# In a two-pass matmul stream, the order of the first few upper and lower products after each change of stage

## Chip, cores and metric

One core of a Trainium2 chip runs the whole kernel. The metric is the device time of one execution in microseconds. A change of under about 0.2% (5 us here) cannot be told from none by a measurement of this kernel.

## What is computed

Two decoder layers on 256 tokens of width 2048, all in float32. The first layer mixes tokens by dilated attention, the second by a gated sum of compressed, selected and windowed attention over shared keys and values. Each is followed by a squared-ReLU MLP of width 8192 and a gated per-layer embedding. Cut to what carries the time:

```python
for i in range(2):
    hn = rmsnorm(h, attn_norm_g[i])
    h = h + (dilated_mixture_attention(hn, a_w_in[i], a_w_out[i]) if i == 0 else
             nsa_attention(hn, b_w_qg[0], b_w_out[0], *shared))   # shared: k/v from rmsnorm(h, kv_norm_g) @ w_kv_shared
    hn = rmsnorm(h, mlp_norm_g[i])
    h = h + square(relu(hn @ mlp_w1[i])) @ mlp_w2[i]               # 2048 -> 8192 -> 2048
    gate = sigmoid(rmsnorm(h, ple_norm_g[i]) @ ple_w_gate[i])
    h = h + (p[i] @ ple_w_proj[i]) * gate
return rmsnorm(h, final_norm_g)
```

## The kernel before

Weights come in chunks of 128 x 1024 float32 (512 KB), one DMA each. ScalarE rounds a chunk to `whi` (L202), VectorE takes the rest, `wlo` = raw - `whi` (L208). Activations are split in the same way, and a tile `xa` (or `oT`, `ko`, `pg`, `h`) holds both parts side by side: 256 columns of upper part, 256 of lower part. A product of float32 accuracy is then made of products of rounded parts, in one of two ways.

- **Feature-major** stages (`quad`, `single`) take a 128 x 128 piece of weights as the stationary operand, twice. `mm_tiles` issues, for each piece, an **upper** product (L332: `whi` against all 512 columns) and a **lower** one (L336: `wlo` against the 256 upper columns). I call the two a pair. With `run=1` they alternate; with `run=2` the order is upper, upper, lower, lower; with `run=8` eight uppers and then eight lowers; with a negative run each lower follows `-run` uppers later. A chunk holds eight pairs.
- **Token-major** stages (`token_major`, L446, L447, L448) take activations as the stationary operand and stream 512 columns of weights in every product, three for each piece.

A `quad` makes four 128-row tiles of output over all its chunks (8 pairs a chunk); a `single` makes one over two chunks. The program is one list of steps, written out in advance; the matmuls run in that order and everything else is placed around them. `prog.op` places a step between chunks.

Where the two kinds of stage meet:

- Mixer A: a unit of values (`v_unit`, token-major, 8 chunks) stands ahead of heads 0, 1, 2, 4 and 5. A head has six tiles by `single` (i = 0 to 5). After the first chunk of tile 1 comes `a_scores` (fp32 products, L748 and L749), after the first chunk of tile 3 `a_transpose` (L777 to L780), and after tile 4 `a_pv` (L800 to L805).
- `out_proj`: four quads in a row, moving operand `oT` or `ko`; the first quad has `a_pv` or `b_pv` steps between its chunks. MLP block 0 follows at once.
- `mlp`: four blocks of 2048 hidden features for each layer; a block is four up-projection quads (256 pairs) and then four token-major down-projection units. Block 0 has the norm's small products after its fifth chunk (L241 and L265). Blocks 1 to 3, called the later blocks here, begin right behind a token-major product.
- Mixer B's sixteen queries: a `single` each, with `b_pv` (L1242 to L1244) and `b_transpose` (L1218) between its two chunks and `b_scores` (L1169 to L1171) behind it.

In the kernel before, three tables choose how a feature-major stage starts after a token-major one. `OPENINGS[layer][block]` is (width of an fp32 product put in front, run of the first chunk, run of the rest); `UNIT_OPENINGS[u]` is (width, run of the first chunk) for the head behind value unit u. `opening(n)` (L356) issues one fp32 product with n columns whose output nobody reads; it shows as two products in the trace.

```python
OPENINGS = (((0, 1, 1), (T, 1, 1), (P, 1, 1), (0, 8, 1)),
            ((0, 1, 1), (0, 2, 1), (0, 2, 2), (0, -1, 1)))
UNIT_OPENINGS = {1: (1, 1), 2: (0, 4), 3: (64, 1), 4: (0, 8)}
```

So block 1 of the first layer opens with a 256-column fp32 product, block 2 with a 128-column one, block 3 with a run of eight; in the second layer block 1 has its first chunk in twos, block 2 all chunks in twos, block 3 the staggered order. Head 1 opens with a 1-column product, head 2 with a run of four, head 4 with a 64-column product, head 5 with a run of eight, and head 0 with nothing.

Of the kernel before, what the change touches and what calls it, by code (L numbers as in the profile page):

```python
# [30 lines left out]
ROPE_SWAP = [(j + 16) % 32 for j in range(32)]  # L31

WARM_UP = 14

OPENINGS = (((0, 1, 1), (T, 1, 1), (P, 1, 1), (0, 8, 1)),
            ((0, 1, 1), (0, 2, 1), (0, 2, 2), (0, -1, 1)))

UNIT_OPENINGS = {1: (1, 1), 2: (0, 4), 3: (64, 1), 4: (0, 8)}
DMA_AHEAD = 7
SPLIT_AHEAD = 3  # L40
RAW_BUFS, HI_BUFS, LO_BUFS = 4, 6, 5
# [96 lines left out]
def kernel(ctx: ExitStack, tc: tile.TileContext, a: dict, out: bass.AP):  # L138
# [185 lines left out]
    def mm_tiles(hi, lo, tiles, run=1):  # L324

        def upper(t):  # L330
            ps, col, rhs, first, _ = t
            nc.tensor.matmul(ps, hi[:, col:col + P], rhs, start=first, stop=False)  # L332

        def lower(t):
            ps, col, rhs, _, last = t
            nc.tensor.matmul(ps[:, :T], lo[:, col:col + P], rhs[:, :T], start=False, stop=last)  # L336

        if run < 0:
            for n, t in enumerate(tiles):
                upper(t)  # L340
                if n + run >= 0:
                    lower(tiles[n + run])
            for t in tiles[run:]:
                lower(t)
            return
        for n in range(0, len(tiles), run):
            for t in tiles[n:n + run]:
                upper(t)
            for t in tiles[n:n + run]:
                lower(t)  # L350

    def opening(n):

        def go():
            ps = banks2()[:, 0, :] if parity[0] else bank()
            nc.tensor.matmul(ps[:, :n], ones, xp[0][:, :n], start=True, stop=True)  # L356
        prog.op(go)

    def sum_halves(ps):
        s = tmp.tile([P, T], F32, tag="es", name="es", bufs=4)  # L360
# [15 lines left out]
            yield  # L376
        yield from g

    def quad(src, nk, acts, done, hooks=None, single_ring=False, late=False, runs=(1, 1)):

        st = []
        for c in range(nk // 2):
            def step(hi, lo, c=c):
                if c == 0:
                    st.extend([bank() for _ in range(4)] if single_ring else four_banks())
                for i in range(2):
                    have(acts, 2 * c + i)
                mm_tiles(hi, lo, [(st[f], i * 512 + f * P, acts[2 * c + i], 2 * c + i == 0, 2 * c + i == nk - 1)
                                  for f in range(4) for i in range(2)], runs[c > 0])
                if c < nk // 2 - 1:  # L390
                    return []
                return [delayed(done(f, st[f]), f // 2 if late else 0) for f in range(4)]
            prog.chunk(src(c), step)
            for fn in (hooks or {}).get(c, ()):
                prog.op(fn)

    def single(src, acts, done, mid=(), ring=bank, one_half=False, run=1):

        st = []
        for c in range(2):  # L400
            def step(hi, lo, c=c):
                if c == 0:
                    st.append(ring())
                tiles = []
                for i in range(8):
                    k = 8 * c + i
                    if one_half:
                        xg, ps = have(acts, k), st[0][:, :T]
                        wh, wl = hi[:, i * P:(i + 1) * P], lo[:, i * P:(i + 1) * P]
                        nc.tensor.matmul(ps, wh, xg[:, :T], start=k == 0, stop=False)  # L410
                        nc.tensor.matmul(ps, wh, xg[:, T:], start=False, stop=False)
                        nc.tensor.matmul(ps, wl, xg[:, :T], start=False, stop=k == KT - 1)
                        continue
                    tiles.append((st[0], i * P, have(acts, k), k == 0, k == KT - 1))
                mm_tiles(hi, lo, tiles, 1 if c else run)
                return [done(st[0])] if c else []
            prog.chunk(src(c), step)
            if c == 0:
                for fn in mid:
                    prog.op(fn)  # L420
# [67 lines left out]
    def out_proj(src, nk, oT, gi, to, norm, hooks, single_ring):  # L488
        for q in range(4):
            def done(f, ps, q=q):  # L490
                add_to_x(4 * q + f, ps)
                yield
                yield from renorm(4 * q + f, gi, to, norm)
            quad(lambda c, q=q: src[q * (nk // 2) + c], nk, oT, done, hooks if q == 0 else None,
                 single_ring and q == 0, True)
            if q == 0 and single_ring:
                prog.op(lambda: parity.__setitem__(0, 1))

    def mlp(layer, xg, norm, to, norm2):

        def down(b, q, ps0, ps1, mm):
            c = slice(q * 512, (q + 1) * 512)
            if b == q == 0:
                cur["y"] = cur["h"].tile([P, 2, D], F32, name=f"y{layer}")
            y = cur["y"]
            for j, ps in enumerate((ps0, ps1)):
                if b:
                    nc.vector.tensor_add(y[:, j, c], ps, y[:, j, c])
                else:
                    nc.scalar.copy(y[:, j, c], ps)  # L510
            if b < NFB - 1:
                return
            yield
            yield "tensor"
            tr = two_banks(not mm)
            for f in range(4):
                for j in range(2):
                    k = 4 * q + f
                    nc.tensor.transpose(tr[f // 2][:, (f % 2 * 2 + j) * P:(f % 2 * 2 + j + 1) * P],
                                        y[:, j, k * P:(k + 1) * P], ident)  # L520
            yield
            for i in range(2):
                nc.vector.tensor_add(xp[2 * q + i], tr[i], xp[2 * q + i])
            for i in range(2):
                yield
                both = [renorm(4 * q + 2 * i + f, G_PLE + layer, to, norm2) for f in range(2)]
                for g in both:
                    next(g)
                yield
                for g in both:  # L530
                    next(g, None)

        for b in range(NFB):
            h = [None] * 16
            fp32, first, rest = OPENINGS[layer][b]
            if fp32:
                opening(fp32)
            for q in range(4):
                def done(f, ps, q=q, h=h):
                    t = sum_halves(ps)  # L540
                    yield
                    while norm.r is None:
                        yield
                    nc.vector.scalar_tensor_tensor(t, t, 0.0, norm.rb, op0=ALU.max, op1=ALU.mult)
                    yield
                    nc.scalar.activation(t, t, AF.Square)
                    ht = cur["h"].tile([P, 2 * T], F32R, tag="h", name="h", bufs=20)
                    yield from split_to(ht, t)
                    h[4 * q + f] = ht
                base = layer * 128 + (b * 4 + q) * 8  # L550
                quad(lambda c, base=base: a["w1"][base + c], KT, xg, done,
                     {4: [norm.factor]} if b == 0 and q == 0 else None, late=True,
                     runs=(rest if q else first, rest))
            for q in range(4):
                base = layer * 128 + (b * 4 + q) * 8
                token_major(lambda c, base=base: a["w2"][base + c], h,
                            lambda ps0, ps1, mm, b=b, q=q: down(b, q, ps0, ps1, mm), whole=True)
# [257 lines left out]
    hooks[4].append(tables)  # L815
    v_unit(0, hooks, banks2)
    prog.op(lambda: nc.vector.tensor_add(pair, ident[:, :64], ident[:, 64:]) and None)
    last_unit = [None]
    for h in range(HA):
        for i in range(6):  # L820
            if i == 0:
                fp32, run = UNIT_OPENINGS.get(last_unit[0], (0, 1))
                last_unit[0] = None
                if fp32:
                    opening(fp32)
            single(lambda c, h=h, i=i: a["w_qk"][(h * 6 + i) * 2 + c], x_a0,
                   lambda ps, h=h, i=i: qk_done(h, i, ps), run=run if i == 0 else 1, mid=
                   [lambda h=h: a_scores(h - 1)] if h and i == 1 else
                   [lambda h=h: a_transpose(h - 1)] if h and i == 3 else
                   [lambda i=i: square_pair(2 * i)] if not h and i < 4 else ())  # L830
# [9 lines left out]
                       7: []})  # L840
        elif u:
            v_unit(u)
            last_unit[0] = u
    out_proj(a["w_oA"], HA, oT, G_MLP, x_m0, n_m0,
             {0: [lambda: a_pv(HA - 2, True)], 1: [lambda: a_pv(HA - 1, True)]}, True)
    prog.op(lambda: close_pool("A"))
# [405 lines left out]
    for h in range(HB):  # L1252
        mid = [lambda h=h: b_pv(h - 4)] if h >= 4 else []
        if h >= 3:
            mid.append(lambda h=h: b_transpose(h - 3))
        single(lambda c, h=h: a["w_q"][2 * h + c], x_a1, lambda ps, h=h: q_done(h, ps), mid)
        if h:
            prog.op(lambda h=h: b_scores(h - 1))
    hooks = {0: [lambda: b_pv(HB - 4, True), lambda: b_transpose(HB - 3)],
# [111 lines left out]
```

## Time and profile before

| | |
|---|---|
| median of 3 runs | 2520.42 us (2520.09 to 2520.87) |
| the profiled execution's own time | 2519.85 us |
| its span, first to last instruction | 2517.8 us |
| granted TensorE clock | 0.999 |
| PE busy | 2506.4 us (100%), 13505 products |
| VectorE busy, ScalarE busy | 1661.9 us (66%), 1351.5 us (54%) |
| DMA | 466.10 MB, 185 GB/s |

In the rows of the timeline the first number is the start of the first instruction in us from the span's start, the second the time from there to the end of the last one; products overlap, so how fast they follow one another is read from the starts. A row of a table by stretches gives the stretch, its length, the time that PE was busy in it with the number of products that touch it, the granted clock, and the DMA engines' share and rate.

### The profile page before, as it was taken

The page shows a single profiled execution, that of the slowest core. Times are in us where ns is not written, and L with a number is a line of the kernel's source. Part 1 is how long each engine was busy: PE and PEld are TensorE (multiplying, and loading weights), DVE is VectorE, ACT ScalarE, POOL GpSimd, SP SyncE. Part 2 cuts the span into 40 slices and gives each one's busy share as a digit, 9 for nine tenths or more (in the row PEclk, how much of TensorE's full clock was granted, in tenths as well). Part 3 has the DMA queues.
Part 4 walks back from the last instruction along what each step waited for, and adds up shares of the span by engine and source line. Part 5 has one row for each costly group of instructions (what it writes and reads, how often), then busy time and mean ns, then how long its engine had stood idle before and what let it go on. Part 6 is the DMA issues. An engine that isn't in the chain of part 4 may idle for free.

```text
span 2517.8 us, 36100 instructions
## 1 busy us (share of the span) xinstructions
PE 2506.4 (100%) x13505; PEld 2160.0 (86%) x13505; DVE 1661.9 (66%) x2808; ACT 1351.5 (54%) x2168; POOL 10.4 (0%) x24
## 2 busy tenths in 40 slices
PE   9999999999999999999999999999999999999998
PEld 8888888888888888888888889888888888888887
DVE  6766677865465565566787989866546556556677
ACT  6444444554454453455564788755545445445455
POOL 0000000000000000000000000000000000000000
PEclk9999999999999999999999999999999999999999
DMA  7555545555555555555555743455555555555553
GB/s 271 171 181 177 176 160 180 176 188 192 190 191 192 191 186 193 190 187 185 190 193 188 245 162 120 142 190 190 192 193 189 193 191 189 192 192 187 184 185 123
DMA packets 130111, 466.10 MB, mean 185 GB/s; under 512 B 14608, under 2 KB 15888, under 8 KB 129936
## 3 DMA queue, kind: packets, MB, share of 16 engines
q1 hardware_dynamic: 129264, 462.68, 53.7%
q8 instruction: 105, 1.72, 0.3%
q0 software_dynamic: 528, 1.07, 0.2%
q14 instruction: 70, 0.57, 0.1%
q10 hardware_dynamic: 144, 0.07, 0.0%
HBM read 461.65 MB, written 2.10 MB: 184 GB/s over the span
## 4 chain that ended last, share of the span: by engine, by line
PE 99%; DVE 0%; DMA 0%; SPq 0%; ACT 0%; issue 0%; DVEq 0%
PE mm L332 22%; PE at L332 17%; PE mm L336 11%; PE at L336 9%; PE mm L448 6%; PE mm L447 6%; PE mm L446 6%; PE at L448 5%; PE at L446 5%; PE at L447 5%; PE at L1218 0%; PE at L749 0%; PE mm L1242 0%; PE mm L976 0%; PE mm L977 0%; DMA raw<-in_w_v 0%
## 5 line engine op out<-in xcount | busy, mean ns | idle before, releaser
L208 DVE TENSOR_TENSOR wlo<-raw,whi 128x1024 fp32r<-128x1024 f32 (+1 forms) x875 | 1065.4, 1219 | 640.3 <-PE at L448 131.6
L202 ACT CAST whi<-raw 128x1024 fp32r<-128x1024 f32 (+1 forms) x875 | 919.9, 1052 | 882.1 <-PE mm L332 204.7
L332 PE MATMUL mm<-xa,whi 128*128 128x512 f32 x2176 | 761.0, 397 | 0.0
L336 PE MATMUL mm<-xa,wlo 128*128 128x256 f32 x2176 | 593.3, 279 | 0.0
L332 PE MATMUL at<-xa,whi 128*128 128x512 f32 x1648 | 572.0, 394 | 0.0
L332 PEld LDWEIGHTS mm<-xa,whi 128*128 128x128 f32 x2176 | 403.6, 188 | 88.4 <-issue 0.4
L336 PE MATMUL at<-xa,wlo 128*128 128x256 f32 x1648 | 450.0, 279 | 0.0
L336 PEld LDWEIGHTS mm<-xa,wlo 128*128 128x128 f32 x2176 | 409.1, 189 | 6.7
L332 PEld LDWEIGHTS at<-xa,whi 128*128 128x128 f32 x1648 | 304.3, 187 | 65.5
L336 PEld LDWEIGHTS at<-xa,wlo 128*128 128x128 f32 x1648 | 310.8, 189 | 5.8
L446 PE MATMUL at<-whi,h 128*128 128x512 f32 x512 | 199.5, 390 | 0.0
L446 PE MATMUL mm<-whi,h 128*128 128x512 f32 x512 | 199.4, 389 | 0.0
L448 PE MATMUL mm<-wlo,h 128*128 128x512 f32 x512 | 199.3, 389 | 0.0
L447 PE MATMUL mm<-whi,h 128*128 128x512 f32 x512 | 199.2, 389 | 0.0
L448 PE MATMUL at<-wlo,h 128*128 128x512 f32 x512 | 199.2, 389 | 0.0
L447 PE MATMUL at<-whi,h 128*128 128x512 f32 x512 | 199.2, 389 | 0.0
L446 PEld LDWEIGHTS mm<-whi,h 128*128 128x128 f32 x512 | 96.1, 188 | 20.0
L448 PEld LDWEIGHTS mm<-wlo,h 128*128 128x128 f32 x512 | 96.1, 188 | 19.9
L448 PEld LDWEIGHTS at<-wlo,h 128*128 128x128 f32 x512 | 96.1, 188 | 19.9
L447 PEld LDWEIGHTS at<-whi,h 128*128 128x128 f32 x512 | 96.1, 188 | 19.9
L446 PEld LDWEIGHTS at<-whi,h 128*128 128x128 f32 x512 | 96.1, 188 | 19.8
L447 PEld LDWEIGHTS mm<-whi,h 128*128 128x128 f32 x512 | 96.1, 188 | 19.7
(317 smaller groups left out, 2533.2 us busy)
## 6 DMA issues: line engine op xcount, KB each, us to landing
raw<-in_w SPq DMA_DIRECT2D x512, 512.0 KB, 3.5
raw<-in_w_qk SPq DMA_DIRECT2D x96, 512.0 KB, 3.5
raw<-in_w_gate SPq DMA_DIRECT2D x56, 512.0 KB, 4.2
raw<-in_w_kv SPq DMA_DIRECT2D x48, 512.0 KB, 4.3
raw<-in_w_v SPq DMA_DIRECT2D x46, 512.0 KB, 3.6
raw<-in_w_q SPq DMA_DIRECT2D x32, 512.0 KB, 4.3
raw<-in_w_oB SPq DMA_DIRECT2D x32, 512.0 KB, 3.6
raw<-in_w_oA SPq DMA_DIRECT2D x16, 512.0 KB, 3.5
```

What stands on the lines that cost most here:

```text
L202: nc.scalar.copy(hi[:, c], t[:, c])
L208: nc.vector.tensor_sub(lo[:, c], t[:, c], f32(hi)[:, c])
L332: nc.tensor.matmul(ps, hi[:, col:col + P], rhs, start=first, stop=False)
L336: nc.tensor.matmul(ps[:, :T], lo[:, col:col + P], rhs[:, :T], start=False, stop=last)
L446: nc.tensor.matmul(st[j], xh, wh, start=k == 0, stop=False)
L447: nc.tensor.matmul(st[j], xl, wh, start=False, stop=False)
L448: nc.tensor.matmul(st[j], xh, wl, start=False, stop=k == KT - 1)
```

## The change

Both tables and `opening` go. The first chunk of blocks 1 to 3 of either MLP runs in twos and all other MLP chunks in ones. The first chunk of tile 0 of heads 0, 1, 2, 4 and 5 runs in twos. In `out_proj` the first chunk of the second quad runs in twos, in both layers. And of mixer B's queries the even ones run both their chunks in twos, through a new argument `both`. Every engine but PE keeps its list of instructions in the same order; on PE the upper and lower products are the same 4272 and 4272 calls, and the four fp32 openings are gone.

```diff
-OPENINGS = (...)
-UNIT_OPENINGS = {...}
+UNIT_AHEAD = (0, 1, 2, 4, 5)
...
     def mm_tiles(hi, lo, tiles, run=1):
...
-        if run < 0:
-            ...
         for n in range(0, len(tiles), run):
-            for t in tiles[n:n + run]:
-                upper(t)
-            for t in tiles[n:n + run]:
-                lower(t)
-    def opening(n):
-        ...
+            for ps, col, rhs, first, last in tiles[n:n + run]:
+                nc.tensor.matmul(ps, hi[:, col:col + P], rhs, start=first, stop=False)
+            for ps, col, rhs, first, last in tiles[n:n + run]:
+                nc.tensor.matmul(ps[:, :T], lo[:, col:col + P], rhs[:, :T], start=False, stop=last)
...
# quad
-                                  for f in range(4) for i in range(2)], runs[c > 0])
+                                  for f in range(4) for i in range(2)], 1 if c else run)
# single
-                mm_tiles(hi, lo, tiles, 1 if c else run)
+                mm_tiles(hi, lo, tiles, run if c == 0 or both else 1)
# out_proj
-                 single_ring and q == 0, True)
+                 single_ring and q == 0, True, 2 if q == 1 else 1)
# mlp
-                     runs=(rest if q else first, rest))
+                     run=2 if b and not q else 1)
# heads of mixer A
-                if fp32:
-                    opening(fp32)
...
-                   lambda ps, h=h, i=i: qk_done(h, i, ps), run=run if i == 0 else 1, mid=
+                   lambda ps, h=h, i=i: qk_done(h, i, ps), run=2 if i == 0 and h in UNIT_AHEAD else 1, mid=
# queries of mixer B
-        single(lambda c, h=h: a["w_q"][2 * h + c], x_a1, lambda ps, h=h: q_done(h, ps), mid)
+        single(lambda c, h=h: a["w_q"][2 * h + c], x_a1, lambda ps, h=h: q_done(h, ps), mid,
+               run=2 - h % 2, both=True)
```

More of the change, by code (lines that the diff above doesn't have):

```diff
@@ L33 @@
 WARM_UP = 14
-OPENINGS = (((0, 1, 1), (T, 1, 1), (P, 1, 1), (0, 8, 1)),
-            ((0, 1, 1), (0, 2, 1), (0, 2, 2), (0, -1, 1)))
-UNIT_OPENINGS = {1: (1, 1), 2: (0, 4), 3: (64, 1), 4: (0, 8)}
+UNIT_AHEAD = (0, 1, 2, 4, 5)
 DMA_AHEAD = 7
@@ L324, in mm_tiles @@
     def mm_tiles(hi, lo, tiles, run=1):
[L330 to L336, printed above, removed]
-        if run < 0:
-            for n, t in enumerate(tiles):
-                upper(t)
-                if n + run >= 0:
-                    lower(tiles[n + run])
-            for t in tiles[run:]:
-                lower(t)
-            return
-        for n in range(0, len(tiles), run):
-            for t in tiles[n:n + run]:
-                upper(t)
-            for t in tiles[n:n + run]:
-                lower(t)
-    def opening(n):
[L354 to L357, printed above, removed]
+        for n in range(0, len(tiles), run):
+            for ps, col, rhs, first, last in tiles[n:n + run]:
+                nc.tensor.matmul(ps, hi[:, col:col + P], rhs, start=first, stop=False)
+            for ps, col, rhs, first, last in tiles[n:n + run]:
+                nc.tensor.matmul(ps[:, :T], lo[:, col:col + P], rhs[:, :T], start=False, stop=last)
     def sum_halves(ps):
@@ L377, in delayed, with quad @@
         yield from g
-    def quad(src, nk, acts, done, hooks=None, single_ring=False, late=False, runs=(1, 1)):
+    def quad(src, nk, acts, done, hooks=None, single_ring=False, late=False, run=1):
         st = []
@@ L395, in quad, with single @@
                 prog.op(fn)
-    def single(src, acts, done, mid=(), ring=bank, one_half=False, run=1):
+    def single(src, acts, done, mid=(), ring=bank, one_half=False, run=1, both=False):
         st = []
@@ L534, in mlp @@
             h = [None] * 16
-            fp32, first, rest = OPENINGS[layer][b]
-            if fp32:
-                opening(fp32)
             for q in range(4):
@@ L817 @@
     prog.op(lambda: nc.vector.tensor_add(pair, ident[:, :64], ident[:, 64:]) and None)
-    last_unit = [None]
     for h in range(HA):
         for i in range(6):
[L821 to L825, printed above, removed]
             single(lambda c, h=h, i=i: a["w_qk"][(h * 6 + i) * 2 + c], x_a0,
-                   lambda ps, h=h, i=i: qk_done(h, i, ps), run=run if i == 0 else 1, mid=
+                   lambda ps, h=h, i=i: qk_done(h, i, ps), run=2 if i == 0 and h in UNIT_AHEAD else 1, mid=
                    [lambda h=h: a_scores(h - 1)] if h and i == 1 else
@@ L842 @@
             v_unit(u)
-            last_unit[0] = u
     out_proj(a["w_oA"], HA, oT, G_MLP, x_m0, n_m0,
```

## The prediction

> **What bounds the kernel now.** I read the page's busy table first, then the list of waits on PE.
>
> ```profile
> PE 2506.4 (100%) x13505; PEld 2160.0 (86%) x13505; DVE 1661.9 (66%) x2808; ACT 1351.5 (54%) x2168; POOL 10.4 (0%) x24
> ```
> ```profile
> PE mm L681 <- DVE ones L174: 1.1, 1, 1.1
> PE at L448 <- DVE wlo L208: 0.5, 1, 0.5
> ```
>
> PE is never without work: its two longest waits in the whole execution are 1.1 and 0.5 us, once each. So no wait can be removed, and nothing that the other engines do faster would count. What is left is how closely products follow one another. A busy PE says nothing about that, so the third view is the table by stretches, one stretch for each later MLP block, from the start of the last L448 product ahead of it to the start of the first L446 product behind it.
>
> ```profile
> 666.72:756.14 89.42, 89.42 (x516) 1.00 0.55 189
> 843.00:933.90 90.90, 90.90 (x516) 1.00 0.54 186
> 1020.72:1111.35 90.63, 90.63 (x515) 1.00 0.54 187
> 1869.78:1958.75 88.97, 88.97 (x514) 1.00 0.55 190
> 2045.58:2134.97 89.39, 89.39 (x515) 1.00 0.56 189
> 2221.79:2312.45 90.66, 90.66 (x514) 1.00 0.55 187
> sum 539.97, PE 539.97; mean PE 90.00
> ```
>
> The six do the same 256 pairs on tiles of the same shapes, at the same granted clock (1.00), yet take 88.97 to 90.90 us. The differences follow the way each starts. The fourth row is block 1 of the second layer, the one whose first chunk already runs in twos. Without the 0.23 us of its last L448 it makes 88.74 / 256 = 0.3466 us a pair. The last row (staggered start) makes 90.43 / 256 = 0.3533. These are two rhythms that each keep going to the end of the block once they have begun: chunk borders, quads and the change from the `mm` to the `at` banks don't break them. I call them fast and slow. The third row (run of eight) and the second (128-column opening) are slow as well. The first (256-column opening) is fast, and its 0.45 us over the fourth row is what its opening costs. The fifth has all chunks in twos: (89.39 - 0.23) / 256 = 0.3483, so twos themselves are not the fastest order; what pays is one chunk of them, and ones after it.
>
> The timeline shows the two starts in twos, and one opening:
>
> ```profile
> 1869.78 0.39 PE L448 MATMUL at<-wlo,h 128*128 128x512 f32 x1
> 1870.00 0.61 PE L332 MATMUL mm<-xa,whi 128*128 128x512 f32 x2
> 1870.46 0.40 PE L336 MATMUL mm<-xa,wlo 128*128 128x256 f32 x2
> 1870.69 0.63 PE L332 MATMUL mm<-xa,whi 128*128 128x512 f32 x2
> ...
> 1872.78 0.40 PE L332 MATMUL mm<-xa,whi 128*128 128x512 f32 x1
> ```
> ```profile
> 2045.58 0.39 PE L448 MATMUL at<-wlo,h 128*128 128x512 f32 x1
> 2045.80 0.62 PE L332 MATMUL mm<-xa,whi 128*128 128x512 f32 x2
> 2046.26 0.40 PE L336 MATMUL mm<-xa,wlo 128*128 128x256 f32 x2
> ```
> ```profile
> 843.00 0.40 PE L448 MATMUL at<-wlo,h 128*128 128x512 f32 x1
> 843.23 0.38 PE L356 MATMUL mm<-x,ones 128*128 128x128 f32 x2
> 843.37 0.48 PE L332 MATMUL mm<-xa,whi 128*128 128x512 f32 x1
> 843.68 0.28 PE L336 MATMUL mm<-xa,wlo 128*128 128x256 f32 x1
> ```
>
> Read the starts: both starts in twos go 0.22, 0.46 us. The same start gives the same steps, so I take the rhythm for a consequence of the order at the start and not of chance. Eight pairs in twos take 1872.78 - 1870.00 = 2.78 us. The opening stands for 843.37 - 843.23 = 0.14 us, and the upper behind it for 0.31 where one behind an L448 takes 0.23 or so (in the first listing, half of the 0.46 of two).
>
> **The change part by part.** *The later MLP blocks.* All six get the order of the fourth row, behind the same kind of stage, from the same ring of banks, over the same sixteen `xa` buffers. 6 x 88.97 = 533.82 against 539.97: **-6.15 us**. The new order asks for the first `wlo` one product later than before, so it adds no wait; PE's list is the only one that changes. The cover for the faster pace is in the fourth row too: DMA brought 190 GB/s there and PE did not wait. If VectorE or the DMAs fell behind, it would show first there, and it does not.
>
> *The five heads behind a value unit.* Stretches from the last L448 to the head's first score product (24 pairs), and for head 0 to its norm (72 pairs):
>
> ```profile
> 85.74:94.66 8.92, 8.92 (x52) 1.00 0.74 247
> 145.88:154.44 8.56, 8.56 (x50) 1.00 0.50 183
> 243.93:252.85 8.92, 8.92 (x53) 1.00 0.49 174
> 304.07:312.72 8.65, 8.65 (x51) 1.00 0.50 180
> 29.21:54.87 25.66, 25.66 (x146) 1.00 0.73 243
> ```
>
> In twos and then fast ones, 24 pairs take 0.23 + 2.78 + 16 x 0.3466 = 8.56, which the run of four (head 2) has already. So head 1 and 4 gain 0.36 each, head 5 gains 0.09, head 2 nothing. Head 0 gets 0.23 + 2.78 + 64 x 0.3466 = 25.19, a gain of 0.47. Together **-1.3 us**. All eight pairs of a head write one bank, those of the MLP four; I cost that at nothing, since the run of eight came out slow from one bank (head 5: 8.42 / 24 = 0.351) and from four.
>
> *What follows in a head.* The fp32 score and transpose products break the rhythm, and which one comes after depends on what stood before, in a way that the trace shows but I cannot derive:
>
> ```profile
> 168.41:176.81 8.40, 8.40 (x51) 1.00 0.50 178
> 206.39:214.96 8.57, 8.57 (x52) 1.00 0.51 174
> 178.55:192.43 13.88, 13.88 (x83) 1.00 0.45 156
> 374.95:389.08 14.13, 14.13 (x82) 1.00 0.42 152
> ```
>
> These are the 24 pairs behind the transposes of heads 2 (fast) and 3 (slow), and the 40 behind a later value product, fast and slow. If heads 1, 2, 4 and 5 all turned slow there, it would cost 4 x 0.17 + 2 x 0.25 + 2 x 0.1 (sixteen pairs at 0.0067) = +1.4; if heads 3 and 6 turned fast, -0.7. I take **0**, for four of the six are fast now.
>
> *The second output quad, and mixer B's queries.* Neither start has a counterpart before.
>
> ```profile
> 452.00:489.00 37.00, 37.00 (x214) 1.00 0.52 183
> 1625.50:1693.00 67.50, 67.50 (x386) 1.00 0.57 191
> 495.00:504.00 9.00, 9.00 (x53) 1.00 0.53 181
> ```
>
> Two products of each count overlap the ends, so the pace is 37.0 / 106 = 0.349 a pair in the first output projection, 67.5 / 192 = 0.3516 in the second, and 9.0 / 25.5 = 0.353 in the first chunks of the MLP behind it. The change can touch 96, 192 and twice 40 pairs. All of them fast: 96 x 0.0024 + 192 x 0.005 + 80 x 0.0064 = -1.7. All slow: 96 x 0.0043 + 192 x 0.0017 = +0.7. Since these paces are neither of the two, something in `oT` and `ko` as operands keeps disturbing the rhythm, and a good start would soon be lost: I take **-0.2**.
>
> ```profile
> 1455.24:1461.00 5.76, 5.76 (x33) 1.00 0.83 261
> 1471.91:1474.78 2.87, 2.87 (x18) 1.00 0.48 176
> 1475.05:1477.98 2.93, 2.93 (x18) 1.00 0.16 32
> 1488.63:1491.45 2.82, 2.82 (x19) 1.00 0.20 83
> 1493.41:1496.27 2.86, 2.86 (x19) 1.00 0.53 180
> ```
>
> These are both chunks of query 0 (16 pairs), the two of query 2, the two of query 4. A chunk in twos takes 2.78, or about 2.86 behind the transposes, where the first upper follows an fp32 product as behind an opening (+0.08). Query 0: -0.20; query 2: -0.16; queries 4 to 14: some 0.03 each, -0.2. Sum **-0.5**. Should twos lock slow there, 8 x 0.3533 = 2.83 makes +0.05 in 16 chunks, +0.3 in all; should the odd queries gain 0.04 a chunk as well, -1.1.
>
> **Sum.** -6.15 - 1.3 + 0 - 0.2 - 0.5 = -8.2, from the profiled execution's 2519.85 (span 2517.8 and 2.05 outside it, which doesn't change) to 2511.7. The median of the runs, 2520.42, stands 0.57 above that execution, so I predict 2512.2. The bounds of the three open terms reach 2.8 below it (0.7 + 1.5 + 0.6) and 3.1 above (1.4 + 0.9 + 0.8).
>
> A rule speaks against all of this. The Trainium skill, "TensorE: Matmul & The Clock Gate", section "Back-to-back issue gap", gives a warm product N / 2.4 + 2.5 ns after the one before, whatever the order: 215.8 + 109.2 = 325 ns a pair, an estimate from that page. The trace disagrees: 346.6 in one block and 353.3 in another of the same shapes.
>
> **Rivals.** *The order does not matter and the rhythm is set elsewhere* (by that rule, for one). Then only the openings go: 3 x (0.14 + 0.08) + 0.45 = 1.1, and the median is 2519.3. Against it stand six blocks with one work and different times. Chance 0.04.
>
> *The start in twos locks fast in some blocks only*, because the fourth row owes its rhythm to something else that it starts with. Each block that turns slow costs 90.66 - 88.97 = 1.69. With two slow the gain falls to 4.8 us, under 0.2% (5.04 us, about what a measurement can tell from none); with three, to 3.1: 2515.6 to 2517.3. Against it: the start in twos of the fifth row runs through the same steps. Chance 0.08.
>
> *Slower than before:* the start in twos locks slow everywhere else, as one run of eight did in two places. Six blocks at 90.66 make 543.96, +4.0; heads at 0.3533 make 0.23 + 24 x 0.3533 = 8.71 and -0.2 in sum, head 0 none. That is 2523.7 on the profiled scale, 2524.2 on the median's, and 2525.2 with the bad bounds of queries and output quads. From five slow blocks on the whole gain is gone (8.2 / 1.69 = 4.9). Chance 0.04.
>
> **How the numbers follow.** My forecast has 0.80, and 0.04 is left for mixtures such as one slow block, still faster. Range: 2509.4 (the good bounds) to 2516.0 (the bad bounds at 2515.3, and two slow blocks). Faster by over 0.2% (below 2515.4): 0.80 and most of the mixtures, with a part of the second rival, 0.86. Within: the rest of that rival, the first, and most of the third, 0.12. Slower by over 0.2%: 0.02.
>
> **What would show it.** Right: six blocks of 88.97, whatever their layer; first chunks at 0.22, 0.46; scores of heads 1 and 4 8.56 after the last L448; no PE wait longer than before. Wrong: a later block near 90.66 with the same first chunk, which would make the rhythm depend on more than the order; queries in twos above 2.83 a chunk; a wait of PE on `whi` or `wlo` inside a block.

## The result and the profile after

The median fell from 2520.27 to 2513.70 us (10 runs each), a ratio of 0.9974 with a 95% interval of 0.9966 to 0.9983: 6.6 us faster, where 8.2 was forecast. The profiled span went from 2517.8 to 2511.3.

The busy table after says as little as before; the waits on PE are the same few:

```profile
PE 2500.4 (100%) x13497; PEld 2156.5 (86%) x13497; DVE 1662.3 (66%) x2808; ACT 1351.0 (54%) x2168; POOL 10.4 (0%) x24
```
```profile
PE mm L650 <- DVE ones L170: 1.1, 1, 1.1
PE at L420 <- DVE wlo L204: 0.4, 1, 0.4
PE at L1131 <- DVE ko L450: 0.3, 1, 0.3
```

There are eight products fewer (the four openings, two records each) and no new wait. Lines have moved: L327 and L329 are now the upper and lower product, L418 to L420 the token-major ones. The table by stretches for the six later MLP blocks, with the same ends as before:

```profile
666.60:755.58 88.98, 88.98 (x515) 1.00 0.58 190
842.40:931.38 88.98, 88.98 (x515) 1.00 0.59 190
1018.20:1107.18 88.98, 88.98 (x515) 1.00 0.59 190
1865.40:1954.38 88.98, 88.98 (x515) 1.00 0.58 190
2041.20:2130.18 88.98, 88.98 (x515) 1.00 0.59 190
2217.00:2305.98 88.98, 88.98 (x515) 1.00 0.59 190
sum 533.88, PE 533.88; mean PE 88.98
```

All six take the same time to the last digit: 539.97 - 533.88 = 6.09 us gained. The five other traces below whose later blocks start in twos show 88.98 in all six blocks as well. The timeline shows the start of twos in block 3 of the first layer, upper pair 0.23 behind the last L420 and first lower 0.45 behind that:

```profile
1018.20 0.39 PE L420 MATMUL at<-wlo,h 128*128 128x512 f32 x1
1018.43 0.61 PE L327 MATMUL mm<-xa,whi 128*128 128x512 f32 x2
1018.88 0.40 PE L329 MATMUL mm<-xa,wlo 128*128 128x256 f32 x2
```

The rest of the span moved little. By stretches between token-major stages: head 0, -0.57; heads 1 to 7 together, 0.0; the first output projection with MLP block 0 behind it, +0.37; the queries and the second output projection with its MLP block 0, -0.25. The zero of heads 1 to 7 hides two things. The 24 pairs ahead of the scores take 8.55 in heads 1, 2, 4 and 5, as forecast (first row: head 1). But the 32 pairs behind the scores take 11.50 (heads 1, 2, 4 and 5; two rows shown), where heads 3 and 6, which have no start in twos, keep 11.29:

```profile
85.24:93.79 8.55, 8.55 (x50) 1.00 0.78 260
95.57:107.07 11.50, 11.50 (x67) 1.00 0.43 148
155.56:167.06 11.50, 11.50 (x67) 1.00 0.43 154
193.75:205.04 11.29, 11.29 (x66) 1.00 0.42 146
```

Before, the same 32 pairs took 11.28 in those four heads; the rows of before for heads 1 and 2:

```profile
96.44:107.72 11.28, 11.28 (x66) 1.00 0.42 143
156.22:167.50 11.28, 11.28 (x66) 1.00 0.40 146
```

Four times 0.22 is 0.9 us given back right behind the gain.

### The profile page after: what moved, and what is told of

Same layout as the page of the kernel before. It is cut to its first block, busy times and chain, and to the rows that moved or that the text cites. A ratio compares the mean times of both kernels' runs of the same rounds, so it can differ in the third digit from the quotient of the medians.

```text
span 2511.3 us, 36082 instructions
## 1 busy us (share of the span) xinstructions
PE 2500.4 (100%) x13497; PEld 2156.5 (86%) x13497; DVE 1662.3 (66%) x2808; ACT 1351.0 (54%) x2168; POOL 10.4 (0%) x24
## 4 chain that ended last, share of the span: by engine, by line
PE 99%; DVE 0%; DMA 0%; SPq 0%; ACT 0%; issue 0%; DVEq 0%
PE mm L327 22%; PE at L327 17%; PE mm L329 11%; PE at L329 9%; PE mm L418 6%; PE mm L420 6%; PE mm L419 6%; PE at L420 5%; PE at L418 5%; PE at L419 5%; PE at L1180 0%; PE at L718 0%; PE mm L1204 0%; PE mm L938 0%; PE mm L939 0%; DMA raw<-in_w_v 0%
## 5 line engine op out<-in xcount | busy, mean ns | idle before, releaser
L327 PE MATMUL mm<-xa,whi 128*128 128x512 f32 x2176 | 756.4, 396 | 0.0
L329 PE MATMUL mm<-xa,wlo 128*128 128x256 f32 x2176 | 587.9, 278 | 0.0
L327 PE MATMUL at<-xa,whi 128*128 128x512 f32 x1648 | 573.7, 393 | 0.0
L327 PEld LDWEIGHTS mm<-xa,whi 128*128 128x128 f32 x2176 | 401.4, 188 | 85.1 <-issue 0.4
L329 PE MATMUL at<-xa,wlo 128*128 128x256 f32 x1648 | 458.5, 278 | 0.0
L329 PEld LDWEIGHTS mm<-xa,wlo 128*128 128x128 f32 x2176 | 409.4, 188 | 9.7
L327 PEld LDWEIGHTS at<-xa,whi 128*128 128x128 f32 x1648 | 308.7, 187 | 70.0
L329 PEld LDWEIGHTS at<-xa,wlo 128*128 128x128 f32 x1648 | 310.2, 188 | 0.1
L418 PE MATMUL at<-whi,h 128*128 128x512 f32 x512 | 199.5, 390 | 0.0
L418 PE MATMUL mm<-whi,h 128*128 128x512 f32 x512 | 199.4, 389 | 0.0
L420 PE MATMUL mm<-wlo,h 128*128 128x512 f32 x512 | 199.2, 389 | 0.0
L420 PE MATMUL at<-wlo,h 128*128 128x512 f32 x512 | 199.2, 389 | 0.0
L420 PEld LDWEIGHTS at<-wlo,h 128*128 128x128 f32 x512 | 96.1, 188 | 20.0
L420 PEld LDWEIGHTS mm<-wlo,h 128*128 128x128 f32 x512 | 96.1, 188 | 20.0
L418 PEld LDWEIGHTS mm<-whi,h 128*128 128x128 f32 x512 | 96.1, 188 | 19.9
L418 PEld LDWEIGHTS at<-whi,h 128*128 128x128 f32 x512 | 96.1, 188 | 19.8
```

The source lines that it names most:

```text
L418: nc.tensor.matmul(st[j], xh, wh, start=k == 0, stop=False)
L420: nc.tensor.matmul(st[j], xh, wl, start=False, stop=k == KT - 1)
```

## The experiments

My theory: a stream of alternating uppers and lowers repeats one of a few cycles, the order of the first products decides which, and the cycle lasts until another kind of product breaks in. The runs below were made on several chips, so their times are compared by the distance from the kernel before on the same chip (the kernel after: -6.6 us). Their intervals reach 2 to 3.4 us to either side, so a smaller difference between two variants rests on the stretches of the traces and not on the medians.

**Ones at the start of the blocks.** Is it the order, or the absence of the openings?

```diff
# mlp
-                     run=2 if b and not q else 1)
+                     run=1)
```

> The kernel after, but the later MLP blocks start in ones like all their other chunks, with no opening. Theory (the order of the first chunk sets a rhythm that lasts to the end of the block): all six blocks lock slow as head 0 did before, 0.23 + 256 x 0.3533 = 90.7 us each instead of 88.98, so +10 us, 2523.9. Rival (the gain came from taking the fp32 openings out): the blocks stay at 88.98 and the time at 2513.7.

Measured: 2523.89 against 2519.72, ratio 1.0016 (1.0007 to 1.0025): +4.2 us, slower than before, and 10.7 from the kernel after. First and last of the six blocks:

```profile
666.88:757.54 90.66, 90.66 (x514) 1.00 0.57 187
2225.85:2316.51 90.66, 90.66 (x514) 1.00 0.57 187
```

All six are slow, 10.1 us in the traces. The openings' removal is not what gains: without an opening and without twos, every block is slow.

**Which groups lock fast.** One kernel, another start in each later block and each head:

```diff
+MLP_RUNS = {(0, 1, 0): (2, 2, 2, 1), (0, 2, 1): 2, (0, 3, 0): (2, 1),      # (layer, block, quad): group sizes, last repeated
+            (1, 1, 0): (4, 1), (1, 2, 0): (2, 2, 1), (1, 3, 0): (3, 3, 2)}
+HEAD_RUNS = {(0, 0): 4, (1, 0): 4, (2, 0): (2, 2, 1), (4, 0): (4, 1), (5, 0): (2, 1)}
```

> The kernel after with another order at the start of each later MLP block, the rest of the block in ones. First layer: block 1 three groups of two; block 2 ones, and the first chunk of its second quad in twos; block 3 one group of two. Second layer: block 1 one group of four; block 2 two groups of two; block 3 threes (3, 3, 2). Heads 0 and 1 start with fours, head 2 with two groups of two, head 4 with one group of four, head 5 with one group of two. Theory: what decides is where in its cycle the last group leaves the stream. In the trace of after the lowers of a group end on 0.119 us after the first and third group and on 0.112 after the second and fourth, so an even number of groups of two locks fast and an odd number slow: first layer 90.6, about 89.4 (64 slow pairs and then fast ones), 90.6; second layer 90.6 (one group of four), 88.98, and no forecast for threes. Heads 0, 1 and 2 fast, 4 and 5 slow. Rival (any group at the start locks fast, since it only has to delay the first lower product): 88.98 in all blocks with a group at the start. Time by the theory about 2519, by the rival about 2514.5.

Measured: 2523.01 us in one run. The six blocks in order, then heads 2, 4 and 5 (the pairs ahead of the scores; these three rows begin with the first upper, 0.23 us later than the rows above, so 8.32 stands for 8.55):

```profile
668.04:758.68 90.64, 90.64 (x515) 1.00 0.56 187
845.55:936.18 90.63, 90.63 (x515) 1.00 0.58 187
1023.05:1113.72 90.67, 90.67 (x515) 1.00 0.57 187
1871.99:1962.63 90.64, 90.64 (x514) 1.00 0.57 187
2049.47:2138.44 88.97, 88.97 (x514) 1.00 0.59 190
2225.26:2315.91 90.65, 90.65 (x515) 1.00 0.57 187
...
145.71:154.03 8.32, 8.32 (x50) 1.00 0.54 182
244.35:252.81 8.46, 8.46 (x50) 1.00 0.54 182
304.54:313.00 8.46, 8.46 (x50) 1.00 0.53 180
```

Behind a token-major product, one and three groups of two lock slow, two groups fast; one group of four slow. With four groups of two (the kernel after) fast, and one of eight (before) slow, that is the rule that was written down: even fast, odd slow. Two groups of three and one of two, an odd number though of mixed sizes, are slow as well; ones, with no group at all, are slow too (the run before). The rival, any group will do, has fallen. One forecast missed: block 2 of the first layer was to change to fast when its second quad began in twos. It stayed slow (90.63, not 89.4). Twos choose a cycle behind a token-major product; out of a running slow cycle they did not lead in this block.

The time missed by 4 us: five blocks are slow where the theory had named three and a part of a fourth (2.9 us), and the heads lost 1.3, above all behind their transposes. There the order of the products does not decide alone. Up to the transposes of head 1 and beyond, the PE products of this run and of the next one (fours in the heads) come in the same order, and the 32 pairs behind the scores took 11.29 and 11.28 us; but the last lower ahead of the transposes took 119 ns to the next start here and 115 ns there, and the 24 pairs behind them ran slow here and fast there (first row: this run; second: the next):

```profile
107.94:116.51 8.57, 8.57 (x51) 1.00 0.51 179
```
```profile
107.53:115.94 8.41, 8.41 (x52) 1.00 0.56 181
```

What made the 4 ns is not known.

**Fours in the heads.**

```diff
-                   ..., run=2 if i == 0 and h in UNIT_AHEAD else 1, mid=
+                   ..., run=4 if i == 0 and h in UNIT_AHEAD else 1, mid=
```

> The kernel after, with fours instead of twos in the first chunk of tile 0 of heads 0, 1, 2, 4 and 5. Theory: the 32 pairs behind the scores of heads 1, 2, 4 and 5 took 11.50 us after and 11.28 before, because the pairs ahead of the scores stop at another place of their cycle; fours leave the cycle that head 2 had before, and the 32 pairs go back to 11.28: 4 x -0.22 = -0.9 us, 2512.8. Rival (it is the lack of an opening, or the faster pace as such, that makes the pairs behind the scores slow): 11.50 stays and so does the time.

Measured: 2512.41 against 2519.72, ratio 0.9970 (0.9957 to 0.9982): -7.3, 0.7 beyond the kernel after; the stretches of the heads in the two traces differ by the same 0.7. The 32 pairs behind the scores of heads 1, 2 and 5:

```profile
95.35:106.63 11.28, 11.28 (x67) 1.00 0.43 143
155.13:166.41 11.28, 11.28 (x67) 1.00 0.43 150
312.94:324.22 11.28, 11.28 (x66) 1.00 0.44 150
```

Fours gain as much ahead of the scores (8.33 us against 8.32 for the 24 pairs of head 1) and lose nothing behind them. So the loss was neither the pace nor the missing opening, but the place in the cycle at which the scores cut in. The ten traces bear that out: over heads 1 to 7 of each, 11.50 us stands behind the scores wherever the last lower ahead of them took 113 or 114 ns to the next start, and never where it took 117 to 121. After fours the steps from start to start are 230 and 117 ns in turn, so no lower is short; after twos they are 231, 112, 233, 117, 231, 113, 232 and 118 ns in turn, at the same mean pace.

**Output quads in ones.**

```diff
-                 single_ring and q == 0, True, 2 if q == 1 else 1)
+                 single_ring and q == 0, True)
```

> The kernel after, with the second output quad in ones in both layers. Theory (twos there moved the stream of the first output projection from 0.349 to 0.353 a pair): the 152 pairs from the third chunk on go from 53.58 back to 53.21 us, the 248 of the second layer stay at 87.2, in all -0.4 us, 2513.3. Rival (those pairs are slower because something upstream, the last heads, hands over another state): they stay at 53.58 and the time at 2513.7.

Measured: 2512.77 against 2519.72, ratio 0.9972 (0.9961 to 0.9983): -7.0. The 152 pairs from the third chunk of the first output projection on (112 of it, then the first 40 of MLP block 0), in this kernel and in the kernel after:

```profile
451.23:504.44 53.21, 53.21 (x307) 1.00 0.55 180
```
```profile
450.40:503.98 53.58, 53.58 (x307) 1.00 0.55 179
```

The twos of the second quad cost 0.37 us in the first layer. In the second layer, over 248 such pairs, they gain 0.04 (87.24 to 87.20), nothing.

**Everything in eights.** If alternation is what has a bad cycle, avoid it.

```diff
# mm_tiles
+        run = len(tiles) or 1
         for n in range(0, len(tiles), run):
```

> The kernel after, with every chunk of every feature-major stage in eights: eight uppers, then eight lowers. Theory: slow and fast are two cycles of an alternating stream; within eights a lower follows a lower 0.120 us behind and an upper an upper 0.227 behind (block 3 of the first layer and head 5 before show both), together 0.3467 a pair, which is the fast pace, and no cycle is left that a start could put wrong. Over 0.3467 a pair the feature-major stretches of after stand 10.9 us in all, of which the first uppers behind fp32 products keep some 6; so -4 to -5 us, about 2509. Rival (eights cost more at each change between uppers and lowers, as twos do with 0.3483 a pair): the fast blocks lose, at +0.2 us or more each, and the time is 2513 or above. Second rival (the operands oT and ko disturb any order): the output projections keep their 53.6 and 87.2 us and the gain is about 2.5.

Measured: 2519.16 against 2519.89, ratio 0.9998 (0.9989 to 1.0007): -0.7. The theory of this run was wrong and its first rival right. Two blocks and the 152 pairs; then the timeline at the start of a block:

```profile
666.83:756.41 89.58, 89.58 (x514) 1.00 0.58 189
2221.95:2311.53 89.58, 89.58 (x514) 1.00 0.58 189
451.08:503.69 52.61, 52.61 (x307) 1.00 0.55 180
```
```profile
667.05 1.98 PE L328 MATMUL mm<-xa,whi 128*128 128x512 f32 x8
668.87 1.11 PE L330 MATMUL mm<-xa,wlo 128*128 128x256 f32 x8
669.82 2.00 PE L328 MATMUL mm<-xa,whi 128*128 128x512 f32 x8
671.66 1.12 PE L330 MATMUL mm<-xa,wlo 128*128 128x256 f32 x8
672.61 0.63 PE L328 MATMUL mm<-xa,whi 128*128 128x512 f32 x2
```

The first chunk takes 669.82 - 667.05 = 2.77, the second 2.79: each later return from lowers to uppers costs 0.02 us, 0.3490 a pair in the whole block. That is better than the slow cycle and worse than the fast one, and it is the same in all six blocks. They lose 0.60 each, 3.6 of the 5.9 us between this run and the kernel after; most of the rest went in other stretches that had run fast, such as the last 192 pairs of MLP block 0 (67.23 against 66.75 in each layer). In the output projections eights gain: 52.61 against 53.21 in ones, 86.68 against 87.24. So the second rival, by which the operands `oT` and `ko` would keep them at 53.6 and 87.2, fell too.

**Two parts together.** Fours in the heads and the output quads in ones.

> The kernel after with fours in the five heads and the output quads in ones, the two changes of the runs before in one kernel. Theory: both act on their own stretches, because the token-major stages between them set the state anew: -0.7 and -0.4 us, 2512.6 beside 2513.7. Rival: the heads' state reaches the output projection, and the two gains do not add.

Measured: 2512.19 against 2519.89, ratio 0.9969 (0.9958 to 0.9980): -7.7, the sum of -0.7 and -0.4 beside -6.6. The stretches agree with those of the two single runs to 0.01 us; they add.

**Queries in ones.**

```diff
-               run=2 - h % 2, both=True)
+               run=1)
```

> The kernel after with mixer B's queries in ones again. Theory: the stretch from the gates to the end of the output projection goes back from 328.3 to 328.5, +0.2 us, as the comparison of before and after has it; the forecast had put -0.5 on the twos there. Rival (the twos brought the forecast 0.5 and something else in the stretch took 0.3 back): +0.5.

Measured: 2513.53 against 2519.89, ratio 0.9976 (0.9967 to 0.9985): -6.4. The stretch from the gates through queries and second output projection to the end of the up-projection of MLP block 0, here and in the kernel after (second fence, first row):

```profile
1451.15:1779.70 328.55, 328.07 (x2017) 1.00 0.49 159
```
```profile
1450.23:1778.55 328.32, 327.77 (x2017) 1.00 0.50 160
1489.08:1491.96 2.88, 2.88 (x20) 1.00 0.55 175
```

The twos are worth 0.23 here. Between traces with the same order of the queries this stretch differs by up to 0.07, most of it in the first two queries, so the size is not known more closely than 0.2 to 0.3. The last row is the second chunk of query 4: 2.88 in twos, not the 2.86 that I had put there.

**A better version.** Fours in the heads, eights in the output projections, and fours behind the transposes of heads 3 and 6.

```diff
-                   ..., run=2 if i == 0 and h in UNIT_AHEAD else 1, mid=
+                   ..., run=4 if i == 0 and h in UNIT_AHEAD else 1,
+                   second=4 if i == 3 and h in (3, 6) else 1, mid=
...
-                 single_ring and q == 0, True, 2 if q == 1 else 1)
+                 single_ring and q == 0, True, 8, 8)
```

> Fours in the five heads, and also in the second chunk of tile 3 of heads 3 and 6 (behind the transposes, where the stream locks slow); both output projections all in eights, where the all-eights kernel took 52.60 and 86.68 us against 53.21 and 87.24 in ones. Everything else as in the kernel after. Theory: -0.7 (heads) and about -1.1 (projections, first quads included a little more) and -0.5 (24 and 16, 24 and 40 pairs back at 0.3467), about 2511 beside 2513.7 for the kernel after. Rival: the start of MLP block 0 takes over a bad state from the eights and gives the projections' gain back; and fours behind an fp32 transpose lock slow, since the rule for groups was found behind token-major products.

Measured: 2511.19 against 2519.97, ratio 0.9965 (0.9951 to 0.9978): -8.8, the best of all, 2.2 beyond the kernel after (by the spans of the traces 2.1). Two rows: the 152 pairs, and the 24 behind the transposes of head 3.

```profile
449.63:502.14 52.51, 52.51 (x306) 1.00 0.55 180
205.65:214.18 8.53, 8.53 (x51) 1.00 0.55 180
```

The eights' gain in the projection stands, and MLP block 0 takes over no bad state: its first 40 pairs in the first layer even turned fast, 13.87 us against 14.13 in the kernel after, while those of the second layer stayed at 14.12. Fours behind an fp32 transpose do not lock fast: 8.53 against 8.56, and the pairs that follow stay at 0.353. An even number of groups is a rule for entering behind token-major products and no more than that. That the forecast time was met is partly luck: heads 3 and 6 gave 0.06 us of the 0.5, and the projections 0.2 more than their 1.1.

## Why the prediction was right, and where its sizes were off

- *The bound.* Right: no wait on PE changed, and the whole gain is closer spacing of the same products.
- *The later MLP blocks.* -6.15 forecast, -6.09 measured. The step that carried it, that the same order behind the same kind of stage gives the same rhythm, held in all six blocks and two layers; the run with ones shows that the order does it, and not the missing openings.
- *The heads.* Head 0: -0.47 forecast, -0.57 found, the rest of it behind its norm. The 24 pairs of the others: 8.56 forecast, 8.55 found. But "What follows in a head" was taken at 0 with the wrong place in view. I priced the pairs behind the transposes, and those did not change (8.41 in head 1, 8.56 in head 3). The loss came two stages earlier, behind the scores: +0.22 in four heads. The row for those pairs was there before and I had not asked what would happen to it. Fours give it back, so this step is 0.9 of the 1.6 us that were missing (head 0 returned 0.1 of it). That the 0.9 lies inside the +1.4 allowed for this term is luck, since the 1.4 was reckoned from pairs that did not change.
- *The second output quad.* -0.2 forecast, +0.33 measured (+0.37 and -0.04), inside the bounds of that term. I had argued that the operands would wipe out any start. In the second layer nothing changed, which agrees; in the first layer the twos moved the stream to 0.353 a pair and it stayed there, and the output quads in ones, which give the 0.37 back, show that the twos did it.
- *The queries.* -0.5 forecast, -0.23 measured. I counted a chunk in twos behind transposes at 2.86, its cost behind a token-major product plus 0.08; it takes 2.88, no less than ones.
- *The rivals.* None came true. That no order could matter is refuted by the run with ones: the same products take 88.98 or 90.66 us. The formula that the prediction took from the Trainium skill, "TensorE: Matmul & The Clock Gate", section "Back-to-back issue gap", has no place for an order, but the section gives it for an isolated matmul and says that in a stream of weight loads and matmuls both set the spacing; so it was a weaker witness against the forecast than the prediction made it. Neither rhythm, 346.7 or 353.3 ns a pair, meets it. The third rival's price was right: six blocks at 90.66 stand 4.0 us above the kernel before.

What stays open is why there are a slow and a fast cycle. The slow one is in the trace of the run with ones: the steps from start to start are 113, 233, 117, 241, 120 and 236 ns, over and over, 1060 ns for three pairs where three fast pairs take 1040. So it loses 0.02 us every three pairs, and eights lose 0.02 once in eight pairs; that suggests one kind of slip that occurs at different rates. No run here shows what slips. It is also open what else than the order acts behind fp32 transposes, where head 1 ran both ways with one order, and why `oT` and `ko` run at paces of their own.

## What to carry to other kernels

Where PE is always busy, compare equal stretches of the same work by length. Two lengths at one clock, as here, can mean that the stream has more than one steady rhythm, and then it is worth trying the order of the few products at its start. Start orders have to be tried at each kind of border, since an order that locked fast behind one kind of product here did not do so behind another or in mid-stream. Look beyond the next break as well, because the pace of what follows can depend on where the cycle was cut. Where the fast cycle could not be reached here, groups of eight gave a pace between the two.

## What the runs showed of the hardware that I had not expected

- A rhythm set by the first four to eight pairs lasts through the 256 pairs of a block (88.7 us), across chunk borders and banks; the six blocks of the kernel after agree to 0.01 us.
- Behind a token-major product, two or four groups of two lock fast, and one or three slow (88.97 or 88.98 us a block, and 90.64 to 90.67).
- State passes through the fp32 scores: with the same six score products in between, the 32 pairs behind them took 11.28 or 11.50 us, after a last lower of 117 ns or more and of 113 or 114 ns ahead of the scores.
- Behind the fp32 transposes the order alone does not settle the rhythm: with one order, 24 pairs took 8.57 us in one trace and 8.41 in another.
